# A decoder layer on eight cores: last FFN half by token parts, and another order of the FFN weights' write-backs

## The chip, the cores and the metric

The kernel runs on all 8 cores of one Trainium2 chip. Each core computes 4096 tokens of its own, in eight tiles of 512 tokens, after four tiles of halo. The metric is the time of the slowest core in microseconds (us), the median of the fast runs. A run is "slow" when one die takes over 1% longer than the other at a lower clock, or when the run is over 1.5% above the fastest of the same kernel. TensorE's clock record says which share of the full clock was granted, so a "0.5 piece" is a stretch at half clock.

## The reference

```python
def reference(x, mem, ...):
    h = rmsnorm(x, g_mix);  proj = h @ w_in           # q, k, v, u, qm
    y = concat(dilated window attention, causal pooling, attention into memory tokens)
    x = x + y @ w_out
    h2 = rmsnorm(x, g_ffn)
    a = relu(h2 @ w_ff1)                              # 1024 -> 4096
    x = x + (a * a) @ w_ff2                           # 4096 -> 1024
    return rmsnorm(x, g_final)
```

## The kernel before

Weights are 1 MB bf16 "pieces" in a ring of three slots. In HBM they are float32 (2 MB a piece). A piece that has not been written back is loaded by a casting load on GpSimd's queue; in one chosen tile the bf16 result is also written back to scratch; later tiles load the 1 MB from scratch on SyncE's queue. `turn` says in which own tile (0 to 3) a piece is written back. A piece with turn t is thus cast t+1 times.

```python
turn = dict(zip([FF1 0..3] + [FF2 0..3] + [FF1 4..7] + [FF2 4..7],     # shortened
                [2, 1, 3, 2, 1, 0, 3, 2, 1, 3, 1, 2, 3, 0, 2, 1]))

def ring_issue():
    n = rs["issued"]
    ...
    s, (idx, j) = n % NRING, seq[n]
    rs["issued"] = n + 1
    if idx in done:
        T.dma("sp", ring_sem[s], ring[s][:], sc[idx], reads=[b_scp[idx]], writes=[b_ring[s]])
        return
    T.dma("pool", cast_sem[s], ring[s][:], wall[idx], writes=[b_ring[s]])
    if turn.get(idx, 0) == j - NHALO:
        done.add(idx)
        T.dma("sp", wb_sem[s], sc[idx], ring[s][:], reads=[b_ring[s]], writes=[b_scp[idx]])
```

Every tile runs stage I (output projection, and the next tile's input projections) and stage K (FF1 and FF2 in two halves of 16 groups each, with the next tile's attention in between). The next x tile, the `X<-xh` load of 2 MB, stands in GpSimd's program order at the end of stage I. Its squares are on ScalarE, among stage K's work:

```python
side += [(23.4, lambda j=j: load_x("pool", (j + 1) % 2, xh[j + 2]))]     # stage I
...
a2 = stage_A(j + 2)
side += ln_side(a2, 6.2, 2, 33.5, 35.2, 1.2)                             # stage K
```

The last FF2 half is 8 groups of 16 matmuls of 512 columns. Behind each group come an add on VectorE, a square and a gain on ScalarE, and the sum of squares on VectorE. The statistics, eight scales and eight stores follow the last group:

```python
side += [(50 + 2 * d + 0.5, lambda d=d: fin.square(d)) for d in range(8)]
side += [(51 + 2 * d, lambda d=d: fin.gain(d, True)) for d in range(8)]
...
fin.stat()                      # one matmul with ones, Ln, Exp
for k in ...: fin.scale(k)      # 5 on VectorE, 3 on GpSimd
for k in ...: T.dma(...)        # 8 stores of 256 KB
```

The softmax here doesn't subtract the row's maximum and nothing guards it: scores larger than these inputs give would overflow.

Of the kernel before, what the change touches and what calls it, by code (L numbers as in the profile page):

```python
# [10 lines left out]
ALU = mybir.AluOpType  # L11
# [14 lines left out]
P_FF2 = 14  # L26
P_KVM = 22
NPIECES = 23
G_MIX, G_FFN, G_FIN, G_MEM = 0, 1, 2, 3
# [78 lines left out]
def build_nc(n_own=NOWN, races=False):  # L108
# [20 lines left out]
    with ExitStack() as es:  # L129
# [11 lines left out]
        def bufs(name, n):  # L141
            return [Buf(f"{name}{i}") for i in range(n)]
# [148 lines left out]
        def write_back(pi):  # L291
            if pi == P_Q:
                T.dma("sp", qwb_sem, sc[pi], aT_lo, reads=b_aT[0:8], writes=[b_scp[pi]])
            else:
# [7 lines left out]
        done = {P_V, P_K, P_UM, P_Q}  # L302
        turn = dict(zip([P_FF1 + i for i in range(4)] + [P_FF2 + i for i in range(4)]
                        + [P_FF1 + 4 + i for i in range(4)] + [P_FF2 + 4 + i for i in range(4)],
                        [2, 1, 3, 2, 1, 0, 3, 2, 1, 3, 1, 2, 3, 0, 2, 1]))
        for j in range(NHALO, NT):
            seq += [(P_WOUT, j), (P_WOUT + 1, j)]
            if NHALO < j < NT - 1:
                seq += [(P_V, j), (P_K, j), (P_Q, j), (P_UM, j)]
            for h in range(2):  # L310
                seq += [(P_FF1 + 4 * h + i, j) for i in range(4)] + [(P_FF2 + 4 * h + i, j) for i in range(4)]
        rs = dict(issued=3, taken=3)

        def ring_issue():
# [13 lines left out]
        def ring_take(expect):  # L328
            n = rs["taken"]
            assert seq[n][0] == expect, (n, seq[n], expect)  # L330
            assert rs["issued"] > n
            rs["taken"] = n + 1
            return ring[n % NRING], b_ring[n % NRING]
# [410 lines left out]
                return f  # L744
            return [group(d) for d in range(8)]

        def stage_K(j, late=None):

            xi, bxi = X[j % 2], b_X[j % 2]
            groups = []  # L750
            st = {}
            R = [(rt[i][:, 0:TOK], [b_rt[i]]) for i in range(2)]
            if late is not None:
                R += [(Pbuf[i][:].rearrange("p h t -> p (h t)").bitcast(F32), [b_P[i]]) for i in range(NPB)]
                R += [(val[:], b_val), (den[:], b_den)]

            def ff1(f_):
                def f():
                    if f_ % 4 == 0:
                        piece, b_ = ring_take(P_FF1 + f_ // 4)  # L760
                        st["p"] = (piece[:].rearrange("p (k c) -> p k c", k=8), b_)
                    pk, bp = st["p"]
                    m_, bm_ = next_mm()
                    c0 = (f_ % 4) * 128
                    mm_ops(m_[:], bm_, [(pk[:, k, c0:c0 + 128], h2T[:, k, :], [bp, b_h2T[k]]) for k in range(8)])
                    r_, br_ = R[cnt["rt"] % len(R)]
                    cnt["rt"] += 1
                    T.op("act", lambda: nc.scalar.activation(out=r_, in_=m_[:], func=AF.Relu), reads=[bm_], writes=br_)  # L768
                    a_ = f_ % 16

                    def finish():
                        if late is not None:
                            T.op("dve", lambda: nc.vector.tensor_tensor(out=r_, in0=r_, in1=late.acc, op=ALU.mult),
                                 reads=late.b_acc, writes=br_)
                        T.op("dve", lambda: nc.vector.tensor_tensor(out=aT[:, a_, :], in0=r_, in1=r_, op=ALU.mult),  # L775
                             reads=br_, writes=[b_aT[a_]])

                    if late is not None and f_ < 4:
                        st.setdefault("finish", []).append(finish)
                    else:  # L780
                        for g in st.pop("finish", []):
                            g()
                        finish()
                    if f_ % 4 == 3:
                        ring_issue()
                return f

            def ff2(h, d, part):
                def f():
                    if d % 2 == 0 and part == 0:  # L790
                        piece, b_ = ring_take(P_FF2 + 4 * h + d // 2)
                        st["p"] = (piece[:].rearrange("p (f c) -> p f c", f=16), b_)
                    pf, bp = st["p"]
                    if part == 0:
                        st["m"] = next_mm()
                    m_, bm_ = st["m"]
                    c0 = (d % 2) * 128
                    mm_ops(m_[:], bm_, [(pf[:, f_, c0:c0 + 128], aT[:, f_, :], [bp, b_aT[f_]]) for f_ in range(16)],
                           8 * part, 8 * part + 8)
                    if part == 1:  # L800
                        T.op("dve", lambda: nc.vector.tensor_tensor(out=xi[:, d, :], in0=xi[:, d, :], in1=m_[:], op=ALU.add),  # L801
                             reads=[bm_], writes=[bxi[d]])
                        if d % 2 == 1:
                            ring_issue()
                return f

            for h in range(2):
                groups += [ff1(16 * h + i) for i in range(16)]
                groups += [ff2(h, d, p_) for d in range(8) for p_ in range(2)]
            return groups  # L810

        def store(j, h):
# [4 lines left out]
        def run(groups, side):  # L817

            side = sorted(side, key=lambda t: t[0])
            p = 0  # L820
            for s, g in enumerate(groups):
                while p < len(side) and side[p][0] <= s:
                    side[p][1]()
                    p += 1
                g()
            while p < len(side):
                side[p][1]()
                p += 1
# [130 lines left out]
        for j in range(NHALO, NT):  # L959
            last = j + 1 == NT  # L960

            ln2 = LN(X[j % 2], b_X[j % 2], G_FFN, h2T, b_h2T, ACC[0])
            first = j == NHALO
            nb = None if first or last else stage_B(j + 1)
            groups = stage_I(j) + (tail if first else [] if last else nb[0])
            if first and two:
                read_v2()
            f_ = fin
            if last:
                side = [(d + 1.2, lambda d=d: ln2.gain(d)) for d in range(8)]  # L970
                side += [(d + 1.5, lambda d=d: ln2.square(d)) for d in range(8)]
            else:
                side = [(d + 2, lambda d=d: ln2.square(d)) for d in range(8)]
                side += [(11, ln2.stat)] + [(12 + 0.5 * k, lambda k=k: ln2.norm(k)) for k in range(8)]
                if f_ is not None:
                    side += [(3, f_.stat)] + [(3.5 + k, lambda k=k, f_=f_: f_.norm(k)) for k in range(8)]
                    side += [(7.6, lambda j=j: store(j - 1, 0)), (11.6, lambda j=j: store(j - 1, 1))]
            if j + 2 < NT and not first:
                side += [(23.4, lambda j=j: load_x("pool", (j + 1) % 2, xh[j + 2]))]
            if nb is not None:  # L980
                side += [(23.3, nb[1])]
            run(groups, side)

            fin = LN(X[j % 2], b_X[j % 2], G_FIN, X[j % 2], b_X[j % 2], ACC[1])
            side = [(50 + 2 * d + 0.5, lambda d=d: fin.square(d)) for d in range(8)]
            if not last:
                side += att_side(j + 1, 1.875, -4 if first else 0)
                pst = pool_steps(j + 1)
                side += [(17 + i, f) for i, f in enumerate(pst[:-2])] + [(36.5, pst[-2]), (38.5, pst[-1])]
                if j + 2 < NT:  # L990
                    a2 = stage_A(j + 2)
                    side += ln_side(a2, 6.2, 2, 33.5, 35.2, 1.2)
                side += [(44, lambda j=j: load_x("pool", (j + 1) % 2, xr[j + 1 - NHALO]))]
            if last:
                side += [(1.5, ln2.stat)]
                side += [(51 + 2 * d, lambda d=d: fin.gain(d, True)) for d in range(8)]
                if f_ is not None:
                    side += [(8, f_.stat)] + [(9.5 + k, lambda k=k, f_=f_: f_.norm(k)) for k in range(8)]
                    side += [(14, lambda j=j: store(j - 1, 0)), (18, lambda j=j: store(j - 1, 1))]
            run(stage_K(j, ln2 if last else None), side)  # L1000
        fin.stat()
        for n_, k in enumerate((0, 2, 1, 3, 4, 5, 6, 7)):
            fin.scale(k)
        for n_, k in enumerate((0, 2, 1, 3, 4, 5, 6, 7)):
            T.dma("sp" if n_ % 2 == 0 else "act", last_sem[k], outd[n_own - 1][:, k, :], X[(NT - 1) % 2][:, k, :],
                  reads=[b_X[(NT - 1) % 2][k]])
        for d_ in last_sem:
            nc.sync.wait_ge(d_.sem, d_.val)
        for i in range(2):
# [112 lines left out]
```

## Time and profile before

The three runs took 1623.55 to 1628.05 us, median 1625.96. The profiled execution is another one, of 1639 us; its slowest core, 3, spans 1638.0 us.

| reading of the kernel before | value | view |
|---|---|---|
| TensorE busy, tiles after 990 us | 181 to 183 us of each 185 us | table of stretches |
| chain of waits, share of TensorE | 85% | page, part 4 |
| TensorE waits in the token tiles, core 3 | 3.8, 4.6, 2.6, 2.0 us | timeline |
| last FF2 half, TensorE | 27.8 us | timeline |
| tail after it | 14.9 us | timeline |

The timeline of TensorE on core 3, kernel before: start, length, line, work, and in brackets the idle time just before and who ended it.

```profile
365.17 15.01 PE L350 MATMUL mm<-aT,ring 128*128 128x512 bf16 x61 [3.77 <-DMA ring<-wall]
...
448.13 3.21 PE L350 MATMUL mm<-h2T,ring 128*128 128x512 bf16 x8 [4.57 <-ACT rt L768]
...
635.87 1.89 PE L350 MATMUL mm<-h2T,ring 128*128 128x512 bf16 x8 [2.62 <-ACT rt L768]
...
822.19 2.93 PE L350 MATMUL mm<-h2T,ring 128*128 128x512 bf16 x8 [2.00 <-ACT rt L768]
```

ScalarE's line just before the second of these waits (core 3, kernel before) shows why its result came late: it sat in its own order at a square of the next x tile.

```profile
444.92 0.63 ACT L371 ACTIVATE sq<-X 128x512 f32<-128x512 f32 x1 [5.10 <-DMA X<-xh]
```

The end of the timeline on core 3, kernel before:

```profile
1595.37 27.79 PE L350 MATMUL mm<-aT,ring 128*128 128x512 bf16 x128
...
1623.27 0.69 DVE L801 TENSOR_TENSOR X<-X,mm 128x512 f32<-128x512 f32 x1 [1.18 <-PE mm L350]
...
1628.35 6.29 DVE L407 TENSOR_TENSOR X<-X,acc 128x512 f32<-128x512 f32 x5 [2.81 <-ACT acc L389]
1628.40 5.10 POOL L407 TENSOR_TENSOR X<-X,acc 128x512 f32<-128x512 f32 x3 [82.74 <-ACT acc L389]
```

The half takes 27.79 us, 217 ns a matmul. Then add, square, sum, statistics and eight scales follow one another, and the stores end at 1638.0.

### The profile page before, as it was taken

To read this page: it belongs to the slowest core of one execution; us is meant where nothing else is said; L and a number is where in the kernel's file an instruction comes from. 1 tells how busy PE (TensorE), PEld (TensorE's weight loads), DVE (VectorE), ACT (ScalarE), POOL (GpSimd) and SP (SyncE) were. 2 spreads that over 40 slices of the span, in tenths; PEclk is the share of its full clock that TensorE was granted. 3 is DMA by queue.
4 is the path that set the end of the run, shared out by engine and by line. 5 is a ranking of instruction groups with operands and counts; after the bars stand their busy time and mean duration, and the time that the engine had idled before them with its cause. 6 is when DMAs were issued, how large, how long until landed. Compare 5 with 4: busy or idle time off the path is not lost.

```text
span 1638.0 us, 27926 instructions; the slowest of 8 cores (1605.7 to 1638.0 us)
## 1 busy us (share of the span) xinstructions
PE 1558.9 (95%) x9722; PEld 755.0 (46%) x9722; DVE 944.4 (58%) x1378; ACT 722.9 (44%) x1085; POOL 161.1 (10%) x219
## 2 busy tenths in 40 slices
PE   4989899989899999999999999999999999999996
PEld 1434534544355444544445544544455544544442
DVE  4665555556366555666465565666475565545654
ACT  3645554442445436453354436353354435354222
POOL 3121110010101001000100010000100000000001
PEclk9998788999999999999999999999999999999998
DMA  9767446686978668574765665343833463343542
GB/s 243 178 213 230 116 68 133 110 177 201 219 162 191 182 215 229 149 202 164 234 191 138 217 208 191 129 155 130 295 116 143 155 228 121 128 172 138 186 151 101
DMA packets 43241, 282.93 MB, mean 173 GB/s; under 512 B 5344, under 2 KB 7520, under 8 KB 10976
## 3 DMA queue, kind: packets, MB, share of 16 engines
q0 software_dynamic: 17952, 121.45, 31.0%
q1 hardware_dynamic: 24576, 158.64, 27.7%
q8 instruction: 81, 1.33, 0.3%
q10 hardware_dynamic: 576, 1.05, 0.2%
q14 instruction: 56, 0.46, 0.1%
HBM read 286.69 MB, written 46.92 MB: 204 GB/s over the span
## 4 chain that ended last, share of the span: by engine, by line
PE 85%; DMA 5%; DVE 4%; ACT 3%; issue 3%; POOL 1%; ACTq 0%; DVEq 0%; SPq 0%; POOLq 0%
PE mm L350 73%; PE ob L652 6%; PE sc L629 4%; DMA X<-xh 2%; DMA ring<-wall 2%; PE sc L350 2%; DVE val L663 1%; ACT P L631 1%; ACT rt L768 1%; DVE acc L381 1%; ACT Vd L355 0%; DMA cpc_t<-cpc 0%; DVE aT L775 0%; POOL Vd L268 0%; DVE P L636 0%
## 5 line engine op out<-in xcount | busy, mean ns | idle before, releaser
L350 PE MATMUL mm<-h2T,ring 128*128 128x512 bf16 x2192 | 517.6, 386 | 15.2 <-ACT rt L768 12.7
L350 PE MATMUL mm<-aT,ring 128*128 128x512 bf16 x2048 | 472.0, 382 | 5.4 <-DMA ring<-wall 3.8
L631 ACT ACTIVATE P<-sc 128x1024 bf16<-128x1024 f32 x256 | 247.5, 1023 | 209.2 <-PE sc L629 208.4
L350 PEld LDWEIGHTS mm<-h2T,ring 128*128 128x128 bf16 x2192 | 206.5, 99 | 265.5 <-issue 60.5
L775 DVE TENSOR_TENSOR aT<-rt 128x512 bf16<-128x512 f32 x232 | 184.1, 793 | 214.5 <-ACT rt L768 212.3
L350 PEld LDWEIGHTS mm<-aT,ring 128*128 128x128 bf16 x2048 | 193.4, 98 | 220.7 <-issue 15.5
L768 ACT ACTIVATE rt<-mm 128x512 f32<-128x512 f32 x232 | 138.3, 596 | 240.2 <-PE mm L350 185.9
L636 DVE TENSOR_TENSOR P<-P,E 128x1024 bf16<-128x1024 bf16 x224 | 154.2, 694 | 135.1 <-ACT P L631 134.1
L371 ACT ACTIVATE sq<-X 128x512 f32<-128x512 f32 x196 | 121.8, 627 | 182.6 <-DVE X L801 109.8
L652 PE MATMUL ob<-P,Vd 128*128 128x128 bf16 x1792 | 140.9, 223 | 12.3 <-DVE val L663 11.0
L652 PEld LDWEIGHTS ob<-P,Vd 128*128 128x128 bf16 x1792 | 119.6, 100 | 70.4 <-issue 30.6
L350 PE MATMUL mm<-hT,ring 128*128 128x512 bf16 x672 | 148.2, 380 | 2.7 <-ACT acc L387 2.2
L801 DVE TENSOR_TENSOR X<-X,mm 128x512 f32<-128x512 f32 x128 | 87.7, 685 | 103.4 <-PE mm L350 101.2
L381 DVE TENSOR_TENSOR acc<-acc,sq 128x512 f32<-128x512 f32 x144 | 105.2, 731 | 43.5 <-ACT sq L371 41.8
L667 POOL TENSOR_TENSOR yT<-val,den 128x512 bf16<-128x512 f32 x48 | 63.4, 1321 | 656.7 <-DVE val L663 335.5
L350 PE MATMUL mm<-yT,ring 128*128 128x512 bf16 x512 | 117.2, 389 | 2.2 <-POOL yT L667 1.7
L350 PEld LDWEIGHTS mm<-hT,ring 128*128 128x128 bf16 x672 | 65.4, 98 | 85.5 <-issue 9.5
L350 PEld LDWEIGHTS mm<-yT,ring 128*128 128x128 bf16 x512 | 50.5, 100 | 69.3 <-issue 19.1
L411 DVE SCALAR_TENSOR_TENSOR h2T<-X,gc,acc 128x512 bf16<-128x512 f32 x80 | 56.0, 745 | 35.3 <-ACT acc L389 30.3
L629 PE MATMUL sc<-Q,KT 64*128 64x128 bf16 x1792 | 73.0, 222 | 1.3 <-ACT P L631 1.3
L629 PEld LDWEIGHTS sc<-Q,KT 64*128 64x128 bf16 x1792 | 54.0, 107 | 41.6 <-issue 38.1
L661 ACT ACTIVATE den<-ob 64x512 f32<-64x512 f32 x96 | 56.7, 591 | 30.2 <-PE ob L652 28.3
(108 smaller groups left out, 939.3 us busy)
## 6 DMA issues: line engine op xcount, KB each, us to landing
ring<-wscratch SPq DMA_DIRECT2D x123, 1024.0 KB, 5.9
ring<-wall POOLq DMA_DIRECT2D x48, 1024.0 KB, 9.8
X<-xh POOLq DMA_DIRECT2D x22, 1024.0 KB, 16.4
wscratch<-ring SPq DMA_DIRECT2D x21, 1024.0 KB, 4.7
X<-xr POOLq DMA_DIRECT2D x16, 1024.0 KB, 10.4
out<-X POOLq DMA_DIRECT2D x14, 1024.0 KB, 9.4
vscratch<-Vd POOLq DMA_DIRECT2D x24, 192.0 KB, 7.1
Vd<-vscratch POOLq DMA_DIRECT2D x6, 768.0 KB, 9.8
```

The source lines that it names most:

```text
L350: T.op("pe", lambda: nc.tensor.matmul(out_ap, lhsT=l, rhs=r, start=(i == 0), stop=(i == n - 1)), reads=rd, writes=[b_out], mark=(i == n - 1))
L371: T.op("act", lambda: nc.scalar.activation(out=s_, in_=self.x3[:, k, :], func=AF.Square), reads=[self.b_x[k]], writes=[bs_])
L381: T.op("dve", lambda: nc.vector.tensor_tensor(out=self.acc, in0=self.acc, in1=s_, op=ALU.add), reads=[bs_], writes=self.b_acc)
L629: T.op("pe", lambda: nc.tensor.matmul(o2, lhsT=l[lo:lo + 64], rhs=rr, start=True, stop=True), reads=bt["qk_reads"], writes=[bs_], mark=(i ...
L631: T.op("act", lambda: nc.scalar.activation(out=P_[:], in_=s_[:], func=AF.Exp, scale=0.125), reads=[bs_], writes=[bP_])
L636: T.op("dve", lambda: nc.vector.tensor_tensor(out=Pv, in0=Pv, in1=m, op=ALU.mult), reads=[bP_, b_E, b_E16], writes=[bP_])
L652: T.op("pe", lambda: nc.tensor.matmul(o_, lhsT=l[:, v0:v0 + 128], rhs=r_, start=(bt["first"] and i == 0), stop=(bt["last"] and i == n - 1) ...
L661: T.op("act", lambda: nc.scalar.activation(out=den[lo:lo + 64, :], in_=ob[hh][o2:o2 + 64, :], func=AF.Ln), reads=[b_ob[hh]], writes=[b_den ...
L667: T.op("pool", lambda: nc.gpsimd.tensor_tensor(out=yT[:, ch, :], in0=val[:], in1=den[:], op=ALU.mult), reads=b_den + b_val, writes=[b_yT[ch]])
L768: T.op("act", lambda: nc.scalar.activation(out=r_, in_=m_[:], func=AF.Relu), reads=[bm_], writes=br_)
L775: T.op("dve", lambda: nc.vector.tensor_tensor(out=aT[:, a_, :], in0=r_, in1=r_, op=ALU.mult), reads=br_, writes=[b_aT[a_]])
L801: T.op("dve", lambda: nc.vector.tensor_tensor(out=xi[:, d, :], in0=xi[:, d, :], in1=m_[:], op=ALU.add), reads=[bm_], writes=[bxi[d]])
```

## The change

Here and in the experiments the diffs are shortened: `...` marks what is cut, and some comments are mine. The change has two intents. The first is to shorten the tail: the last FF2 half is done in token parts of 256, 128 and 128 columns, with all four of its weight pieces on chip (three in the ring, the fourth in the free `hT`), so that norm and stores of one part run under the matmuls of the next. The second is another order of write-backs, with FF1 pieces 0 to 2 written back in the very first own tile.

```diff
-                        [2, 1, 3, 2, 1, 0, 3, 2, 1, 3, 1, 2, 3, 0, 2, 1]))
+                        [0, 0, 0, 1, 2, 3, 1, 2, 0, 3, 1, 2, 3, 1, 2, 3]))
...
+        seq.pop()                                   # the last piece is not loaded to the ring
...
+        def load_last():                            # but to hT, at group 33
+            T.dma("sp", last_sem[0], dst, sc[P_FF2 + 7], reads=[...], writes=b_hT)
+        PARTS = [(0, 256), (256, 384), (384, 512)]
...
+            def ff2_part(part, d, lo, hi):
+                    mm_ops(m_[:, 0:hi - lo], bm_, [(pf[:, f_, c0:c0 + 128], aT[:, f_, lo:hi], ...)
+                                                   for f_ in range(16)])
+                    T.op("dve", ... xi[:, d, lo:hi] + m_[:, 0:hi - lo] ...)
...
+                for i, (lo, hi) in enumerate(PARTS):
+                    fl = LN(xl[:, :, lo:hi], b_last[i], G_FIN, None, None, a_, n=hi - lo, early=True)
+                    side += [(48 + 8 * i + d + 1, ... fl.square(d)) for d in range(8)]
+                    side += [(48 + 8 * i + d + 1.1, ... fl.gain(d, True)) for d in range(8)]
+                    # stat, scales and stores of a part stand among the groups of the next part
```

More of the change, by code (lines that the diff above doesn't have):

```diff
@@ L745, in stage_I, with stage_K @@
             return [group(d) for d in range(8)]
-        def stage_K(j, late=None):
+        def load_last():
+            dst = hT[:].rearrange("p a t -> p (a t)")
+            if P_FF2 + 7 in done:
+                T.dma("sp", last_sem[0], dst, sc[P_FF2 + 7], reads=[b_scp[P_FF2 + 7]], writes=b_hT)
+            else:
+                T.dma("pool", kvm_sem, dst, wall[P_FF2 + 7], writes=b_hT)
+        PARTS = [(0, 256), (256, 384), (384, 512)]
+        b_last = [bufs(f"last{i}_", 8) for i in range(len(PARTS))]
+        def stage_K(j, late=None, parts=None):
             xi, bxi = X[j % 2], b_X[j % 2]
@@ L805, in ff2, with f @@
                 return f
+            def ff2_part(part, d, lo, hi):
+                def f():
+                    if part == 0 and d % 2 == 0:
+                        if d == 6:
+                            st[6] = (hT[:].rearrange("p a t -> p (a t)"), b_hT)
+                        else:
+                            piece, b_ = ring_take(P_FF2 + 4 + d // 2)
+                            st[d] = (piece[:], [b_])
+                    pf, bp = st[d - d % 2]
+                    pf = pf.rearrange("p (f c) -> p f c", f=16)
+                    m_, bm_ = next_mm()
+                    c0 = (d % 2) * 128
+                    mm_ops(m_[:, 0:hi - lo], bm_, [(pf[:, f_, c0:c0 + 128], aT[:, f_, lo:hi], bp + [b_aT[f_]])
+                                                   for f_ in range(16)])
+                    T.op("dve", lambda: nc.vector.tensor_tensor(out=xi[:, d, lo:hi], in0=xi[:, d, lo:hi],
+                                                                in1=m_[:, 0:hi - lo], op=ALU.add),
+                         reads=[bm_], writes=[b_last[part][d]])
+                return f
             for h in range(2):
                 groups += [ff1(16 * h + i) for i in range(16)]
-                groups += [ff2(h, d, p_) for d in range(8) for p_ in range(2)]
+                if h == 1 and parts:
+                    groups += [ff2_part(i, d, lo, hi) for i, (lo, hi) in enumerate(parts) for d in range(8)]
+                else:
+                    groups += [ff2(h, d, p_) for d in range(8) for p_ in range(2)]
             return groups
@@ L984, in build_nc @@
             fin = LN(X[j % 2], b_X[j % 2], G_FIN, X[j % 2], b_X[j % 2], ACC[1])
-            side = [(50 + 2 * d + 0.5, lambda d=d: fin.square(d)) for d in range(8)]
+            side = [] if last else [(50 + 2 * d + 0.5, lambda d=d: fin.square(d)) for d in range(8)]
             if not last:
@@ L995, in build_nc, with split, put @@
                 side += [(1.5, ln2.stat)]
-                side += [(51 + 2 * d, lambda d=d: fin.gain(d, True)) for d in range(8)]
+                xl = X[j % 2]
+                def split():
+                    for b_ in b_last:
+                        for d in range(8):
+                            b_[d].w, b_[d].r = b_X[j % 2][d].w, list(b_X[j % 2][d].r)
+                side += [(47.9, split)]
+                tail_out = []
+                for i, (lo, hi) in enumerate(PARTS):
+                    a_ = (acc[1][:, lo:hi], [Buf(f"acclast{i}")])
+                    a_[1][0].r = list(b_acc[1].r)
+                    fl = LN(xl[:, :, lo:hi], b_last[i], G_FIN, None, None, a_, n=hi - lo, early=True)
+                    side += [(48 + 8 * i + d + 1, lambda d=d, fl=fl: fl.square(d)) for d in range(8)]
+                    side += [(48 + 8 * i + d + 1.1, lambda d=d, fl=fl: fl.gain(d, True)) for d in range(8)]
+                    def put(n_, k, i=i, lo=lo, hi=hi):
+                        T.dma("sp" if n_ % 2 == 0 or i + 1 < len(PARTS) else "act", last_sem[k], outd[n_own - 1][:, k, lo:hi], xl[:, k, lo:hi],
+                              reads=[b_last[i][k]])
+                    order = (0, 2, 1, 3, 4, 5, 6, 7)
+                    outs = [fl.stat] + [lambda k=k, fl=fl: fl.scale(k) for k in order]
+                    outs += [lambda n_=n_, k=k, put=put: put(n_, k) for n_, k in enumerate(order)]
+                    if i + 1 < len(PARTS):
+                        at = 48 + 8 * i + 10
+                        side += [(at, outs[0])] + [(at + 0.5 + 0.7 * n_, f) for n_, f in enumerate(outs[1:9])]
+                        side += [(at + 2.5 + 0.7 * n_, f) for n_, f in enumerate(outs[9:])]
+                    else:
+                        tail_out += outs
                 if f_ is not None:
@@ L999, in build_nc @@
                     side += [(14, lambda j=j: store(j - 1, 0)), (18, lambda j=j: store(j - 1, 1))]
-            run(stage_K(j, ln2 if last else None), side)
-        fin.stat()
-        for n_, k in enumerate((0, 2, 1, 3, 4, 5, 6, 7)):
-            fin.scale(k)
-        for n_, k in enumerate((0, 2, 1, 3, 4, 5, 6, 7)):
-            T.dma("sp" if n_ % 2 == 0 else "act", last_sem[k], outd[n_own - 1][:, k, :], X[(NT - 1) % 2][:, k, :],
-                  reads=[b_X[(NT - 1) % 2][k]])
+            if last:
+                side += [(33, load_last)]
+                run(stage_K(j, ln2, PARTS), side)
+            else:
+                run(stage_K(j), side)
+        for f in tail_out:
+            f()
         for d_ in last_sem:
```

## The prediction

> **What bounds it now.** TensorE. In the stretches table of the slowest core (3) it is busy 181 to 183 us of every 185 us tile from 990 us on, at granted clock 1.00. The chain of waits is 85% PE. So time can come only from PE's waits and from the tail after its last FF2 matmul. The timeline shows the big waits of the token tiles on core 3: 3.8 us at 365 (ring<-wall, casting load of an FF2 piece, 20.4 us to landing where 9.8 is the median), 4.6 us at 448, 2.6 at 636 and 2.0 at 822. The 448 one is ScalarE held in order at a square whose X<-xh took 18.7 us to land (ScalarE 5.1 us idle on it), with the core's DMA busy 93%. Core 2 has 1.7, 4.3 and 1.0 us at the same places. The tail runs from 1623.2 (last matmul) to 1638.0: 14.8 us (add 0.70, square 0.64, sum 0.70, stat 1.1, Ln and Exp 1.3, eight scales 6.3, stores 2.2, rest latency).
>
> **Write-backs.** Casting loads of FF pieces fall from 43 to 40 (sum of turn+1). More important is where: FF1 pieces 0 to 2 are written back in the first own tile, when DMA is busy 59%, instead of the second to fourth. At the start of the next tiles' FFN, where X<-xh loads, casts of 2 MB read become 1 MB loads on the other queue, and GpSimd's queue holds no casts in front of the X load. I expect the waits at 448, 636, 822 to shrink by about two thirds (6 us on core 3, 4 on core 2), and the one at 365 by 1 to 2 us, since FF2 piece 5's write-back leaves that window. Gain: about 6 us (4 to 9).
>
> **Split tail.** PE work hardly changes: 8 matmuls of 128x128 take 0.44 us, 56 ns each, against 216 ns at 512 columns, so parts of 256+128+128 columns cost about 28.4 us against 27.8. The page "TensorE: Matmul & The Clock Gate" of the Trainium skill, section "Back-to-back issue gap", gives 81 ns for N=128 in a stream with weight loads; this trace shows 56, and I use 56. But the 128-column parts become bound by VectorE and ScalarE. Estimated from 0.69 us at 512 and 0.42 at 256 columns, a 128-column add or sum is 0.29 us, a square 0.30, a gain 0.38. In program order a group on VectorE is add, wait for the square, sum, scale of the part before: 1.1 to 1.3 us against PE's 0.9. That makes the half about 32.8 us instead of 27.8: 4 to 5 us lost. After the last matmul all steps shrink: about 8 us instead of 14.8 (scales about 2.5; the store's 2.2 stays). VectorE scales run beside GpSimd at 1.26 us against 0.73 alone: the page "SBUF — State Buffer", section "Who interferes with whom", says a VectorE instruction with two SBUF inputs contends with GpSimd reads, and the trace agrees. Net tail gain: about 2 to 4 us of the 7 hoped for. The loads of FF2 pieces are in time (4.8 us to landing against 7 us of work).
>
> **Sum.** 1626 - 6.5 - 3.5 = about 1616 us; range 1607 to 1623. Chances: faster by over 2%: 0.02; within 2%: 0.97; slower: 0.01.
>
> **Right if** the timeline shows waits at 448, 636 and 822 below 2 us; the second half of the last FF2 takes 31 to 34 us of PE with waits released by VectorE X in the 128-column parts; the tail after the last matmul is 7 to 9 us.
>
> **Wrong if** casts packed into the second tile's FFN collide with X<-xr and bring a new ring wait; the granted clock moves (0.85 in 125 to 340 us here); or VectorE keeps pace, which gives 4 us more.

## More of the kernel before

The answer about cores, kernel before: span, and mean granted TensorE clock.

```profile
core 2: 1628.3 us, clock 0.975
core 3: 1638.0 us, clock 0.974
...
core 7: 1605.7 us, clock 0.995
die 0 (median of its cores): 1621.2 us, clock 0.984
die 1 (median of its cores): 1613.9 us, clock 0.992
```

Two neighbouring cores stand out. The clock record in their trace has 0.8125 from 125 to 286 us (but for 3.4 us at 0.5); the six others have no such piece. Core 3 is the slowest of this execution, but it isn't a typical core.

## The result and the profile after

The changed kernel took 1600.26 to 1600.56 us in four fast executions (one more, of 1884.51 us, was slow); the kernel before took 1623.55 to 1628.05 us. The ratio is 0.9844, with an interval of 0.9827 to 0.9861. A ratio here is the mean time of one kernel's fast runs over that of the other's of the same rounds, so it isn't quite the ratio of the medians quoted. The gain of about 25 us lies outside the predicted range, whose best end was 1607 us.

The answer about cores, changed kernel:

```profile
core 2: 1597.9 us, clock 0.996
core 3: 1595.3 us, clock 0.998
...
core 7: 1596.0 us, clock 0.997
```

All eight cores now end between 1595.3 and 1599.5 us. The timeline of TensorE on the slowest core, 4, has one wait over 0.6 us in the token tiles from 315 to 1500 us:

```profile
341.87 8.36 PE L351 MATMUL mm<-aT,ring 128*128 128x512 bf16 x37 [0.77 <-DMA ring<-wall]
```

So the waits at 448, 636 and 822 us are gone, not shortened, and of the one at 365 us (near 343 us on a core at full clock) 0.77 us is left. The end of the timeline on core 4, changed kernel:

```profile
1558.03 1.80 PE L351 MATMUL mm<-aT,ring 128*128 128x256 bf16 x15
...
1579.85 1.05 PE L351 MATMUL mm<-aT,ring 128*128 128x128 bf16 x16 [0.55 <-DVE X L833]
...
1593.32 0.29 DVE L382 TENSOR_TENSOR acc<-acc,P 128x128 f32<-128x128 f32 x1 [0.57 <-ACT P L372]
...
1595.15 1.87 DVE L408 TENSOR_TENSOR X<-X,acc 128x128 f32<-128x128 f32 x5 [1.54 <-ACT acc L390]
```

The half starts at 1558.0 and its last matmul ends at 1591.8: 33.8 us. The last scales take 1.87 us instead of 6.29. From the half's start to the end of the span it is 41.5 us, against 42.7 before. The split thus gained only about 1.2 us, and nearly all of the 25 us has to come from the other part of the change.

### The profile page after: what moved, and what is told of

The parts are those of the page before. It is cut to its first block, busy times and chain, and to the rows that moved or that the text cites. A ratio compares the mean times of both kernels' runs of the same rounds, so it can differ in the third digit from the quotient of the medians.

```text
span 1599.5 us, 28515 instructions; the slowest of 8 cores (1595.3 to 1599.5 us)
## 1 busy us (share of the span) xinstructions
PE 1514.3 (95%) x9819; PEld 761.4 (48%) x9982; DVE 946.0 (59%) x1418; ACT 730.5 (46%) x1121; POOL 160.4 (10%) x222
## 3 DMA queue, kind: packets, MB, share of 16 engines
q1 hardware_dynamic: 27312, 162.58, 29.6%
## 4 chain that ended last, share of the span: by engine, by line
PE 86%; DVE 4%; issue 4%; ACT 3%; DMA 2%; POOL 1%; DVEq 0%; ACTq 0%; SPq 0%; POOLq 0%
PE mm L351 73%; PE ob L653 6%; PE sc L630 4%; DMA ring<-wall 2%; PE sc L351 2%; DVE val L664 1%; ACT P L632 1%; DVE acc L382 1%; ACT rt L779 1%; ACT Vd L356 1%; DMA cpc_t<-cpc 0%; DVE aT L786 0%; POOL Vd L268 0%; DVE P L637 0%; DVE X L833 0%
## 5 line engine op out<-in xcount | busy, mean ns | idle before, releaser
L351 PE MATMUL mm<-h2T,ring 128*128 128x512 bf16 x2123 | 493.1, 380 | 15.5 <-issue 8.1
L351 PE MATMUL mm<-aT,ring 128*128 128x512 bf16 (+2 forms) x2150 | 451.4, 360 | 13.2 <-issue 7.6
L351 PEld LDWEIGHTS mm<-aT,ring 128*128 128x128 bf16 x2208 | 200.0, 98 | 205.2 <-issue 7.0
L372 ACT ACTIVATE sq<-X 128x512 f32<-128x512 f32 (+2 forms) x200 | 120.9, 610 | 152.2 <-DVE X L812 87.8
L812 DVE TENSOR_TENSOR X<-X,mm 128x512 f32<-128x512 f32 x120 | 82.2, 685 | 86.8 <-PE mm L351 84.7
L382 DVE TENSOR_TENSOR acc<-acc,sq 128x512 f32<-128x512 f32 (+2 forms) x144 | 103.1, 716 | 40.4 <-ACT sq L372 38.7
L351 PE MATMUL mm<-yT,ring 128*128 128x512 bf16 x503 | 112.3, 379 | 3.1 <-POOL yT L668 2.1
L412 DVE SCALAR_TENSOR_TENSOR h2T<-X,gc,acc 128x512 bf16<-128x512 f32 x80 | 56.0, 745 | 34.7 <-ACT acc L390 30.9
```

The source lines that it names most:

```text
L351: T.op("pe", lambda: nc.tensor.matmul(out_ap, lhsT=l, rhs=r, start=(i == 0), stop=(i == n - 1)), reads=rd, writes=[b_out], mark=(i == n - 1))
L372: T.op("act", lambda: nc.scalar.activation(out=s_, in_=self.x3[:, k, :], func=AF.Square), reads=[self.b_x[k]], writes=[bs_])
L382: T.op("dve", lambda: nc.vector.tensor_tensor(out=self.acc, in0=self.acc, in1=s_, op=ALU.add), reads=[bs_], writes=self.b_acc)
L812: T.op("dve", lambda: nc.vector.tensor_tensor(out=xi[:, d, :], in0=xi[:, d, :], in1=m_[:], op=ALU.add), reads=[bm_], writes=[bxi[d]])
```

## The experiments

All outputs are right. In the table "waits" is the sum of TensorE's waits over 0.6 us between 300 and 1500 us (one at line 652/653 that every kernel has is left out), and "half clock" is half the length of the clock record's 0.5 pieces in that time. Both are my sums from the trace of one core. "Marker" is where that core meets one wait that these kernels share, in the last tile.

| kernel, core | waits | half clock | marker | span |
|---|---|---|---|---|
| before again, core 2 | 15.7 | 6.8 | 1527.5 | 1622.1 |
| before again, core 5 | 8.9 | 5.1 | 1516.8 | 1612.3 |
| order only, core 2 | 2.4 | 0 | 1507.2 | 1601.9 |
| order only, core 5 | 0 | 0 | 1502.9 | 1598.9 |
| first three only, core 5 | 3.8 | 1.7 | 1510.3 | 1604.9 |
| changed kernel, core 4 | 0.8 | 0 | 1506.0 | 1599.5 |

### The parts of the change alone, and the state of the cores

The first question was whether the 0.81 clock of cores 2 and 3 made the kernel before slow (a state), or the kernel brought it about. The edits: none (e0_before_again), only the `turn` line (e1_order_only), everything but the `turn` line (e2_tail_only), and the changed kernel (e3_after_again).

> The kernel before, unchanged, for a second profile and more runs. Theory A (state): the granted clock of 0.81 on cores 2 and 3 from 124 to 286 us in the first profile is a state of that chip or execution and no property of the kernel; so the pair at 0.81 comes on the same cores or not at all whichever kernel runs, and on cores without it the span is 1605 to 1615 us. Theory B (kernel): the kernel before brings it about in every execution; then this run shows 0.81 pieces of about 160 us on some cores, slowest core 1623 to 1628 us.

Fast runs 1623.2 to 1631.7 us; ratio 1.0019 (0.9989 to 1.0049). The clock record of this profile has no 0.81 piece on any core, yet the slowest core took 1622.1 us. So neither of my two theories fits: the 0.81 clock isn't brought about by this kernel each time, and without it the slowest core is not at 1605 to 1615. It is slow from waits. The timeline of TensorE on core 2, kernel before again:

```profile
345.46 4.87 PE L350 MATMUL mm<-aT,ring 128*128 128x512 bf16 x14 [3.85 <-DMA ring<-wall]
...
428.27 3.25 PE L350 MATMUL mm<-h2T,ring 128*128 128x512 bf16 x8 [4.41 <-ACT rt L768]
...
618.26 3.07 PE L350 MATMUL mm<-h2T,ring 128*128 128x512 bf16 x8 [4.83 <-ACT rt L768]
...
806.28 3.35 PE L350 MATMUL mm<-h2T,ring 128*128 128x512 bf16 x8 [2.56 <-ACT rt L768]
```

Each wait is followed by slow matmuls: 3.07 to 3.35 us for eight that take 1.89 at full clock. The clock record has a piece of 3.4 us at 0.5 beside each of the four.

> Only the order of write-backs is changed. Theory A: the slowest core at granted clock 1.0 gains 8 to 12 us on undisturbed cores of the kernel before (1606 to 1614 down to 1597 to 1602), because each removed PE wait of over 3.5 us also removes a 3.4 us piece at clock 0.5 that costs 1.7 us more; no clock piece of 0.5 between 125 us and the tail. Theory B: if the write-back order is what removes the 0.81 clock, this run shows none and takes about 1601 us while the kernel before keeps 1625. Rival on the size: by my prediction, order alone is worth 6 us.

Fast runs 1602.9 to 1603.8 us, ratio 0.9871 (0.9854 to 0.9888): the order alone gives about 21 us, more than I expected even then. No 0.5 piece is left between 200 us and the tail, on any core. TensorE's waits over 0.6 us on core 2 after 315 us, up to the last tile, are these:

```profile
342.87 7.50 PE L350 MATMUL mm<-aT,ring 128*128 128x512 bf16 x34 [1.61 <-DMA ring<-wall]
...
525.84 1.89 PE L350 MATMUL mm<-aT,ring 128*128 128x512 bf16 x8 [0.75 <-DMA ring<-wall]
```

On core 2 the account closes: waits fell from 15.7 to 2.4 us and half-clock loss from 6.8 to 0, together 20.1 us, and the marker moved by 20.2 us. It is not always so exact: over the eight cores the sum is between 1.1 us below and 4.6 us above what the marker moved. One reason is that a 0.5 piece can begin before the wait has ended, and that part is counted twice.

> Only the split last half; old order of write-backs. Both theories: the half takes 33 to 34 us of PE and the tail after it 7.5 to 8 us, together 1 to 2 us less than before, so 1604 to 1613 us on undisturbed cores, and the waits at 365 and 448 with their 0.5 clock pieces stay. Theory B in its tail form: if the tail is what removes the 0.81 clock, none here.

Fast runs 1622.2 to 1626.0 us, ratio 0.9999 (0.9977 to 1.0021). With the old order the tail gives nothing that these runs resolve. In the trace, half plus tail took 41.5 to 41.6 us on the eight cores, against 42.6 to 44.1 before.

> The changed kernel again. Theory A: 1597 to 1601 us on undisturbed cores on this chip too, and 0.81 pieces on the same cores as the kernel before if the chip gives them. Theory B: never a 0.81 piece in the fast state.

Fast runs 1600.6 to 1602.0 us, no 0.81 piece. Against the order alone on the same chip the tail is worth about 2 us (medians 1601.5 and 1603.1).

So the 0.81 clock doesn't explain the result: the difference stays in executions without it. It came back later, on cores 4 and 5 of another kernel's profile (e12_bf16_in_place), at 125 to 198 and 202 to 286 us, the same times as on cores 2 and 3 of the first. Pieces of 15 us came on cores 0 and 1 at 422 us (e4_early_x) and, in one profile (e7_hold_ladder), on cores 0 and 1 at 203 us and on cores 2 and 3 at 1256 us. Each time in these profiles it fell on a pair of cores.

### What a wait costs: a ladder of deliberate waits

In the changed kernel TensorE was made to wait for chains of small GpSimd instructions, 3 to 18 of them, in the fifth to seventh own tiles.

```diff
+        def hold(n):
+            T.wait("pool", (T.sem["pe"], T.cnt["pe"], "pe"))
+            for _ in range(3 * n):
+                tok = T.op("pool", ... tensor_tensor(scr, scr, scr, add), writes=[b_scr])
+            T.wait("pe", tok)
+            if j in (8, 9, 10):
+                side += [(28.2, ... hold(2 * j - 15)), (40.2, ... hold(2 * j - 14))]
```

> The changed kernel with six deliberate waits of TensorE on GpSimd, of about 1 to 7 us in steps of about 1 us, in the fifth to seventh own tiles. Theory: long waits are followed by one or more pieces of 3.4 us at granted clock 0.5 that cost half their length, short ones by none; the step lies somewhere between 2 and 5 us. Rival: the half clock pieces of the kernel before came from something else than PE's wait; then the ladder shows none. The time rises by the waits plus 1.7 us for each piece.

The timeline of TensorE on core 1 shows five of the six; the shortest left no wait over 0.6 us:

```profile
1046.85 1.01 PE L653 MATMUL ob<-P,Vd 128*128 128x128 bf16 x8 [3.30 <-POOL scr L998]
...
1206.79 0.61 PE L653 MATMUL ob<-P,Vd 128*128 128x128 bf16 x8 [2.98 <-POOL scr L998]
...
1243.03 1.01 PE L653 MATMUL ob<-P,Vd 128*128 128x128 bf16 x8 [5.91 <-POOL scr L998]
...
1406.15 1.01 PE L653 MATMUL ob<-P,Vd 128*128 128x128 bf16 x8 [5.59 <-POOL scr L998]
...
1445.14 1.01 PE L653 MATMUL ob<-P,Vd 128*128 128x128 bf16 x8 [8.40 <-POOL scr L998]
```

The clock record of this core has 0.5 pieces of 3.4, 3.4, 6.8, 6.8 and 10.2 us at these places. The five waits come to 26.2 us and half of the pieces to 15.4, and the marker of this core moved by 41.2 us against the changed kernel's core 1. That this agrees so well is in part luck: 8.3 us of the pieces lie inside the waits, and the core has a 0.81 piece of 15.1 us that the sum leaves out. On the eight cores the sum of waits and half pieces is between 1.4 us below and 5.3 us above what the marker moved. The run was made once (1639.5 us). Waits of 5.6 us and more had pieces of 6.8 us or longer on all eight cores. The rival (pieces from another cause) is out: none of these pieces is in the changed kernel.

Counted over five profiles (both of the kernel before, the two parts alone, the ladder), all cores, between 300 and 1520 us: of 41 waits of 1.0 to 1.9 us none had a 0.5 piece (19 of the 41 are the marker), of 28 waits of 1.98 to 3.0 us 22 had one, and of 77 longer ones all but one. Length isn't all of it: before 300 us, a wait of 2.1 us near 190 us, on 38 of the 40 cores, had a piece on one of them only. The Trainium skill, page "TensorE: Matmul & The Clock Gate", section "HAM oscillation — how this bites in real kernels", describes this: a wait for DMA that crosses an activity window of about 3.4 us sets the clock to half, and what follows starts cold. These traces agree on the half and on the 3.4 us. Between 300 and 1520 us they show the loss already at waits of 2 us.

### Why the order removes the waits: queue place or traffic

I first thought of the queue. In the kernel before, the X<-xh load of the second own tile stands on GpSimd's in-order queue behind three casting loads that wait for ring slots. It is issued at 406.4 us (core 2, before again), against 389.9 and 392.0 us, in two halves, with the new order (core 2, order only). Two experiments moved it, with the old order of write-backs.

```diff
 # e4_early_x
-                side += [(23.4, lambda j=j: load_x("pool", (j + 1) % 2, xh[j + 2]))]
+                side += [(15, lambda j=j: load_x("pool", (j + 1) % 2, xh[j + 2]))]
 # e10_x_on_sp
+                side += [(15, lambda j=j: load_x("sp", (j + 1) % 2, xh[j + 2]))]
```

> The kernel before with the old order of write-backs; only the X<-xh load stands earlier in program order, in front of the casting loads of the FF1 pieces on GpSimd's queue. Same transfers, same write-backs. Theory Q (queue): the waits at 425, 615 and 805 come from the X load standing behind casts that wait for ring slots, 14 to 16 us in the second own tile; then they vanish here, with their pieces at clock 0.5; the wait at 345 stays; slowest core 1604 to 1610 us. Theory T (traffic): they come from DMA traffic of casts and write-backs; then the X load still lands late and the time stays within 5 us of before.

Fast runs 1626.8 to 1629.6 us, ratio 1.0032 (1.0012 to 1.0051): no gain. The wait for X was gone, and in its place TensorE waited for the casts. The timeline of TensorE on core 4:

```profile
408.51 5.27 PE L350 MATMUL mm<-h2T,ring 128*128 128x512 bf16 x16 [5.07 <-DMA ring<-wall]
...
599.91 5.14 PE L350 MATMUL mm<-h2T,ring 128*128 128x512 bf16 x16 [6.00 <-DMA ring<-wall]
...
614.39 5.99 PE L350 MATMUL mm<-h2T,ring 128*128 128x512 bf16 x14 [4.49 <-DMA ring<-wscratch]
```

Theory Q fell in the form in which I had put it. But this kernel held the first cast back too (on core 2, GpSimd waited 10.5 us for an output store before the second half of the X load), so the queue could still be to blame.

> The kernel before, old order of write-backs, with the X<-xh load issued early from SyncE's queue instead of GpSimd's, so that it stands neither behind the casting loads nor in front of them. Same transfers. Theory Q2 (GpSimd's in-order queue has no room for both the X load, that waits for an output store, and the casts): waits at 406 to 425, 600 to 615 and 805 shrink below 1.5 us, the wait at 345 stays, slowest core 1604 to 1611. Theory T (traffic of 2 MB casts and write-backs on shared DMA engines): X or the FF1 pieces still land late, waits of 3 us and more stay, slowest core over 1616.

Fast runs 1635.0 to 1642.0 us, ratio 1.0087 (1.0055 to 1.0120): slower. On core 6 the X load was issued at 379 to 391 us, apart from the casts, which went out at 384.2, 391.1 and 398.0 us, as early as ever. Two casts, those issued at 384.2 and 410.2 us, still ended waits of TensorE, after 15.8 and 16.9 us to landing, where the median is about 10. Later tiles, that have no casts any more, got new waits, since SyncE's queue now stood at the X load while ring loads queued up behind it. On core 2:

```profile
611.03 4.32 PE L350 MATMUL mm<-h2T,ring 128*128 128x512 bf16 x13 [7.59 <-DMA ring<-wscratch]
...
1170.97 4.25 PE L350 MATMUL mm<-h2T,ring 128*128 128x512 bf16 x13 [4.01 <-DMA ring<-wscratch]
```

That is in line with the page "DMA: Bandwidth & Descriptors", section "Issuing engines are not separate DMA queues": transfers of all issuing engines run on the same 16 DMA engines. This kernel has two effects in one, so the next one keeps the queue and changes the bytes. First, the three early pieces alone, as plain loads on SyncE's queue:

```diff
 # e5_first_three
-                        [2, 1, 3, 2, 1, 0, 3, 2, 1, 3, 1, 2, 3, 0, 2, 1]))
+                        [0, 0, 0, 2, 1, 0, 3, 2, 1, 3, 1, 2, 3, 0, 2, 1]))
```

> The old order with only FF1 pieces 0 to 2 written back in the first own tile (37 casts of FF pieces instead of 43). Theory Q: the waits at 425, 615 and 805 vanish as in the order alone, because no cast stands before the X load; the wait at 345 is untouched (3 to 4 us plus 1.7 us of half clock on the cores that have it); slowest core 1604 to 1609 us. If the spread of the later write-backs mattered, it would stay over 1612.

Fast runs 1604.9 to 1606.0 us, ratio 0.9892 (0.9870 to 0.9914). Three numbers of sixteen give about 18 of the order's 21 us. One wait over 1 us is left on core 2 in the tiles before the last one:

```profile
344.58 5.73 PE L350 MATMUL mm<-aT,ring 128*128 128x512 bf16 x18 [3.64 <-DMA ring<-wall]
```

Then the same pieces in bf16, but loaded from the places on GpSimd's queue where the kernel before casts them:

```diff
 # e12_bf16_in_place, on top of e5_first_three
+            if P_FF1 <= idx < P_FF1 + 3 and idx in done and j - NHALO <= (2, 1, 3)[idx - P_FF1]:
+                T.dma("pool", cast_sem[s], ring[s][:], sc[idx], reads=[b_scp[idx]], writes=[b_ring[s]])
+                return
```

> As e5_first_three, but in the tiles in which the kernel before casts FF1 pieces 0 to 2 they are loaded in bf16 from the same place of the same GpSimd queue. So queue order is that of the kernel before, the X<-xh load stands behind them, and only bytes are fewer. Traffic theory: the waits at 425, 615 and 805 vanish or fall below 1.5 us although the X load is issued 14 us later than in e5_first_three; slowest core within 3 us of e5_first_three (1605.6). Queue theory: the X load still lands too late, waits of 3 us and more stay there, slowest core over 1614.

Fast runs 1605.4, 1606.0 and 1606.2 us, and one of 1626.2 us with the 0.81 clock on cores 4 and 5; ratio, with that one, 0.9897 (0.9873 to 0.9920). Without it, it is e5_first_three to within 1 us. The X load still stands behind three loads, 15.0 us after the first of them, as in the kernel before. GpSimd's timeline, kernel before again, core 2:

```profile
391.39 0.54 POOL L100 DMA_DIRECT2D ring<-wall  x1 [4.73 <-PE mm L350]
...
406.39 1.05 POOL L100 DMA_DIRECT2D X<-xh  x2
```

And with bf16 in place, core 2:

```profile
385.51 0.54 POOL L100 DMA_DIRECT2D ring<-wscratch  x1 [5.01 <-PE mm L353]
...
400.50 1.05 POOL L100 DMA_DIRECT2D X<-xh  x2
```

What differs is how long the two X loads then take to land. The tile's answer for X in this stretch, kernel before again and then bf16 in place:

```profile
DMA to landing us min/median/max: 18.6/19.9/21.2
```

```profile
DMA to landing us min/median/max: 8.4/9.7/11.0
```

So less traffic alone is enough. With the casts gone from this stretch, the X load lands in half the time on core 2 (in 10.8 to 14.8 us on cores 0, 3 and 6) and the late issue does no harm. But in the changed order itself the X load isn't late. Its answer for X on core 2 of e1_order_only:

```profile
L100 POOL DMA_DIRECT2D X<-xh x2: 527/530/532, 389.9 to 392.0; - x2
...
DMA to landing us min/median/max: 15.8/17.3/18.8
```

There it takes nearly as long to land as before (17.3 against 19.9 us), and it is in time because it is issued about 15 us earlier, with no cast in front of it (some 4 us of this, because the wait near 345 us is shorter). By these traces both effects are at work in the change; they were not separated with the new order. An early issue without fewer bytes wasn't enough (e4, e10: the casts came late instead); fewer bytes with the late issue were. What e12 takes away is the second megabyte of each cast, the casting itself, and the write-back of FF1 piece 1, which in the kernel before falls into the same stretch (issued at 408.8 us). Which of these weighs most wasn't separated.

```diff
 # e6_ff2_moved: write-backs of FF2 pieces 1 and 5 out of the first own tile
+                        [2, 1, 3, 2, 1, 2, 3, 2, 1, 3, 1, 2, 3, 2, 2, 1]))
```

> The old order with the write-backs of FF2 pieces 1 and 5 moved from the first own tile to the third. Theory: the wait at 345 (3.4 to 3.9 us on four of eight cores) comes from write-back and casts sharing the DMA engines in the dense half; then it shrinks below 1.7 us here while those at 425, 615 and 805 stay, and the slowest core gains 0 to 5 us. Rival: it comes from the casts and the X<-xr load alone, and stays.

Fast runs 1621.4 to 1623.7 us, ratio 1.0003 (0.9974 to 1.0032). The wait at 345 us is gone from all eight cores, so those write-backs did cause it. But nothing is gained; core 2 has larger waits further on:

```profile
423.83 3.57 PE L350 MATMUL mm<-h2T,ring 128*128 128x512 bf16 x8 [6.57 <-ACT rt L768]
...
615.83 2.74 PE L350 MATMUL mm<-h2T,ring 128*128 128x512 bf16 x8 [4.46 <-ACT rt L768]
```

Each of the two pieces is cast in two more tiles here, so the traffic moved rather than left.

### What holds the split half back

The 128-column parts run at 1.06 us a group instead of TensorE's 0.90. Two candidates: the order add, square, sum on VectorE and ScalarE, or TensorE waiting for one of two PSUM banks.

```diff
 # e9_four_banks (also part of e8 and e11): in the last half
+                    MM.extend((ob[i], b_ob[i]) for i in range(2))
 # e8_lagged_sums, e11_two_parts, e13_lag_two_banks: the sum of group d behind the add of d+1
+            def square(self, k):
+                self.flush()                          # emits the sum of the group before
...
+                self.pend = lambda: T.op("dve", ... acc + sq ...)
 # e11_two_parts
+        PARTS = [(0, 384), (384, 512)]
```

> The changed kernel with two things in its split half: the sum of squares of group d is put behind the add of group d+1 on VectorE, and four PSUM banks instead of two. Theory: in the 128-column parts the half is bound by the chain add, square, sum on VectorE and ScalarE in program order (1.06 us a group against 0.9 of TensorE); then the half takes 29 to 31 us instead of 33.8, the tail after it stays 7.5 to 8 us, and the time falls 2.5 to 4.5 us to about 1597. Rival: TensorE waits for PSUM banks alone; then the run with four banks alone gains the same.

> The changed kernel with four PSUM banks instead of two in its split half, nothing else. Chain theory: banks let TensorE run ahead but the chain on VectorE ends no sooner; the last scale comes at the same time within 1 us, time within 1 us of the changed kernel. Rival (banks): 2.5 to 4.5 us faster.

> As e8_lagged_sums with two token parts (384, 128) instead of three. Fewer groups and one norm less in the middle, but scales of 384 columns on VectorE in the last part. Expected within 1.5 us of e8_lagged_sums, 1596 to 1599 us; if the scales of the wide part bind the last part, TensorE waits of over 0.3 us a group show there.

> As e8_lagged_sums with two PSUM banks. If the order on VectorE alone is what binds, half plus tail take within 0.8 us of the 38.1 us of e8_lagged_sums; if both edits are needed, it takes 39.5 us or more.

From traces, on all eight cores:

| kernel | half | after it | sum | fast runs | ratio to before |
|---|---|---|---|---|---|
| before again | 27.8 | 14.8 to 16.3 | 42.6 to 44.1 | 1623.2 to 1631.7 | 1.0019 |
| changed | 33.8 | 7.7 to 7.9 | 41.5 to 41.8 | 1600.3 to 1600.6 | 0.9844 |
| e9, four banks, five cores | 34.3 | 7.7 to 8.0 | 41.9 to 42.2 | 1599.7 to 1600.2 | 0.9849 |
| e9, cores 4, 6 and 7 | 32.6 | 8.7 to 8.9 | 41.3 to 41.5 | 1599.7 to 1600.2 | 0.9849 |
| e13, lag, two banks | 31.8 | 7.2 to 7.3 | 39.0 to 39.1 | 1597.0 to 1597.2 | 0.9843 |
| e8, lag, four banks | 30.9 | 7.2 to 7.3 | 38.1 to 38.2 | 1595.7 to 1597.5 | 0.9830 |
| e11, (384, 128) | 29.6 | 9.5 to 9.8 | 39.1 to 39.4 | 1596.1 to 1599.2 | 0.9836 |

In the changed kernel VectorE idles between an add and its own sum. VectorE's timeline on core 2 of the changed kernel, one group of the second part, 1.06 us from add to add:

```profile
1578.77 0.28 DVE L833 TENSOR_TENSOR X<-X,mm 128x128 f32<-128x128 f32 x1
1578.97 0.42 DVE L408 TENSOR_TENSOR X<-X,acc 128x256 f32<-128x256 f32 x1
1579.62 0.29 DVE L382 TENSOR_TENSOR acc<-acc,sq 128x128 f32<-128x128 f32 x1 [0.24 <-ACT sq L372]
1579.83 0.28 DVE L833 TENSOR_TENSOR X<-X,mm 128x128 f32<-128x128 f32 x1
```

With the sum one group later it doesn't wait. The same on core 2 of e8_lagged_sums:

```profile
1580.14 0.27 DVE L847 TENSOR_TENSOR X<-X,mm 128x128 f32<-128x128 f32 x1
1580.34 0.41 DVE L422 TENSOR_TENSOR X<-X,acc 128x256 f32<-128x256 f32 x1
1580.67 0.28 DVE L393 TENSOR_TENSOR acc<-acc,sq 128x128 f32<-128x128 f32 x1
1580.88 0.28 DVE L847 TENSOR_TENSOR X<-X,ob 128x128 f32<-128x128 f32 x1
```

From add to add it is 0.74 us, so TensorE's 0.90 is the longer one again. The instruction order is most of the 3.4 us that e8 saves (2.5 without the banks). Four banks alone save nothing on five cores and about 0.2 us on three, and once the order is mended they save 0.9 more. My expectation for e13 named 0.8 or less, or 1.4 or more, above e8; it came out between. By its ratio e8_lagged_sums is the best kernel that ran, but its interval (0.9806 to 0.9854) overlaps that of the changed kernel: on different chips, the 3.4 us are shown by the traces and not by the ratios. In two parts the half is shorter still, but the last norm is no smaller, and the tail after it is longer. VectorE, with scales of 384 columns among its adds, ends its last add at 1586.6 us, 2.7 us after TensorE's last matmul (core 2); I had expected no such tail.

## Why the prediction was right or wrong

- **What bounds the kernel** was right: TensorE. But "time can come only from PE's waits and from the tail" left out busy time at half clock, which the change also removed.
- **The write-backs** were the term of the sum that was mis-sized: "Gain: about 6 us (4 to 9)" measured about 21 us. There are three reasons in it. "I expect the waits at 448, 636, 822 to shrink by about two thirds" was too timid: they vanished. The prediction counted waits alone, where most of 2 us or more also cost half of a 3.4 us piece or more at half clock; that is 6.8 us on core 2 of the second profile. These two make up most of it: core 3 of the first profile, from which the prediction was made, had 12.9 us of waits and 5.1 us of half clock by the sums of the table, 18 us in all. The prediction also took its sizes from one profile, whose cores 2 and 3 ran at 0.81 clock for 160 us; core 2 had 7.1 us of waits there (by the same sum) and 15.7 in the second profile. The time is that of the slowest of eight cores, and each core has its own sum of waits.
- **Why the waits vanish**: both reasons given hold. Fewer bytes were enough by themselves, as bf16 loads in the same places show. "GpSimd's queue holds no casts in front of the X load" is also true: in the changed order the X load is issued about 15 us earlier, which makes up most of its earlier landing. Alone, with the old traffic, an earlier issue gained nothing.
- **The wait at 365** shrank by more than the "1 to 2 us" expected, from 3.9 to 1.6 us on core 2, with a half-clock piece of its own. Its cause, write-backs of FF2 pieces in that stretch, was as predicted.
- **The split tail** had its mechanism right and nearly its sizes: a half of 33.8 us (predicted 32.8), 7.7 us after it (predicted 8), released by VectorE's adds. The net of "about 2 to 4 us" measured 1.2 us between the slowest cores of the traces (0.9 to 2.6 over all cores), and about 2 us between two kernels on one chip. Its "1.26 us" for a scale beside GpSimd is a mean of five: three took 1.74 to 1.75 us and two 0.68 to 0.69. The 0.9 us by which the half was longer is a wait that I missed: with 256 columns TensorE reaches the last of `aT` before VectorE has made it (0.90 us at 1560.7 us on core 4, ended by VectorE's `aT`).
- **"Wrong if the granted clock moves"** was listed for the 0.81 clock. The clock that did move was the half clock after waits, visible in the lengths of the very lines that I had read.
- **All three signs under "Right if"** came true, and the total was still wrong. They asked for waits below 2 us and for the sizes of the split half, but not for what the waits had cost.

## What to carry to other kernels

When TensorE waits for about 2 us or more, look at the matmuls behind the wait as well, and in the clock record: here the brackets were only about 70% of the price (15.7 of 22.5 us on core 2). Here a wait on an x tile or a weight in a stretch with full DMA engines wasn't mended by moving one transfer ahead of another or to another queue; try first to take bytes out of the stretch, and check that they don't come back in the next. When work is cut into small parts, write down the in-order loop of every engine over one part, and put a step that waits for another engine behind the next part's work.

## What the Trainium skill lacked or had wrong

- "TensorE: Matmul & The Clock Gate", "HAM oscillation — how this bites in real kernels", gives "no PE-idle gaps >~3.4µs" as the rule. Here, between 300 and 1520 us, 22 of 28 waits of 1.98 to 3.0 us brought a piece of half clock, and none of 41 waits of 1.0 to 1.9 us did.
- The same page, "Seeing it yourself", has the 13/16 clock on a whole die once three of its cores run dense matmuls. In the profiled fast runs, where all eight cores ran dense matmuls, it came on pairs of cores only and in some executions only: for about 160 us near the start on cores 2 and 3 or 4 and 5, and for 15 us on 0 and 1 or 2 and 3, while the other cores of the die had none. The slow runs, in which the means of all four cores of a die fell (0.814 to 0.826 in the changed kernel's), left no trace to tell.
- The same page, "Back-to-back issue gap", gives 81 ns for 128 columns and 131 ns for 512 in a stream with weight loads. Here, in such a stream, it was 56 ns (8 matmuls in 0.44 us) and 217 ns (128 in 27.79 us), which is near what the section gives for an isolated matmul (about 56 and 216 ns).
- "DMA: Bandwidth & Descriptors", "Issuing engines are not separate DMA queues", is borne out as far as moving the X load to another queue gained nothing. The section doesn't say what the choice of queue does cost: a load that waits at the head of SyncE's queue held up the loads behind it, and TensorE by 3.5 to 7.6 us a tile (e10_x_on_sp, core 2).
